# Laying softmax factors along the columns by way of DRAM instead of by transposes, in one layer of a hybrid encoder

## The chip, the cores and the metric

The kernel runs on one core of a Trainium2 chip. A core has five engines with instruction queues of their own: TensorE (matmuls and transposes; PE in the profile, its weight loads PEld), VectorE (DVE), ScalarE (ACT), GpSimd (POOL) and SyncE (SP), which here only issues transfers. Transfers between DRAM and the core's memory run beside the engines, on 16 DMA engines. The metric is the device time of one execution in microseconds (us). A result is the median of several executions.

## The reference

One layer on a sequence of 512 positions and a model width of 1024, batch 1, all in float32:

```python
h = rms_norm(x, attn_norm_g)
xr, gate, q, k, v = split(h @ w_in)
y_rnn = (rg_lru(conv(xr), forward) + rg_lru(conv(xr), backward)) * gelu(gate)
y_attn = dilated_attention(q, k, v, rel_bias)         # 8 heads of width 64
x = x + concat(rms_norm(y_rnn), rms_norm(y_attn)) @ w_out
x = x + square(relu(rms_norm(x) @ w_up)) @ w_down
return rms_norm(x)
```

The dilated attention has three windows with different strides; the outputs of the three are combined by the denominators of their softmaxes. That is the same as one softmax over all 512 keys with a bias per distance that counts how many windows hold the key. For each head and each query, the sum of the exponentials is the denominator; its reciprocal is the softmax factor that this change is about.

## The kernel before

**Matmuls.** Every float32 matmul is done as three: both operands are split into a rounded part and a remainder (`..h`/`hi` and `..l`/`lo`), and high x high, high x low and low x high are added (`mm3`, lines 303 to 305). Weights come in chunks of 128 x 1024: a transfer fills one of three buffers `wraw` (line 234, issued by SyncE), ScalarE makes `whi` (line 251), VectorE the remainder `wlo` (line 259), and the next `wraw` load goes out when the buffer is free.

**Stages.** Input projection with the recurrent group's gates and scans (to about 90 us); the attention loop, with the rest of the projections and the first half of the output projection woven in (to about 192 us); the second half of the output projection (to about 219 us); then the up and down projections in two halves, with products saved by sums and differences of blocks, and the final norm.

**The attention loop** (lines 1009 to 1041) goes over `i` from 0 to 4 and over four query blocks `u`. Heads are taken in pairs, `p` = 0 to 3. In step `i`, TensorE computes the scores of pair `i` (`att_s`, tiles `ps`; lines 754, 755) and turns the exponentials of pair `i-1` (`att_t`, tiles `pt`, line 778). VectorE adds the bias to the scores and takes the minimum (`att_e`, line 767), ScalarE takes the exponential and the sum over the keys (line 768). The bias comes from `tw` tiles, loaded by `load_tw` (line 450). Between these, `fill` runs "fillers": the key and query projections of the later pairs (tiles `pqk`) and then the output projection of the recurrent group (tiles `pwo`). The products with the values (`att_av`, tiles `pav`, line 859) run for pair 0 at the start of `i` = 2, for pairs 1 and 2 at the start of `i` = 4, and for pair 3 after the loop.

**The softmax factors.** `att_e` gathers the sums of the exponentials of a pair in a tile of 128 x 8: the query within its block is the partition, and the eight columns are four blocks times two heads. The products `pav` lie the other way: the 64 value columns of each of the two heads are the partitions, and the 512 queries the columns. So the factors must be laid along the columns and repeated over 64 partitions. Before, that is done so:

- `att_z` (at `u` = 0, lines 789 and 791): VectorE takes the reciprocal `rz` and repeats each of its columns 64 times, `rzb`, 128 x 512.
- `att_r` (at `u` = 1, lines 382 and 798): TensorE transposes `rzb` in four pieces into one PSUM bank, `prow`, and ScalarE copies it to `zrow`.
- `att_av` (line 863): VectorE multiplies `pav` by `zrow`, tile `yp`. For pairs other than 2, `att_q` and `att_a` follow at once on ScalarE; for pair 2 they come later by a plan (`att_a` at `i` = 4, `u` = 1).

**What sets the order.** TensorE, VectorE, ScalarE and GpSimd run their instructions in the order of the program's statements. SyncE does not: its transfers are ordered by the framework's planner, which sends them as what they need is expected to be ready, and SyncE then runs its queue in that order, waiting at each for its semaphores. Tiles of 128 x 512 come from a pool of 48 (`g_`); small ones from pools of 8.

At the end of the key projections, in step `i` = 2, `load_x` sends the residual (`x`, eight transfers) and the pre-added blocks of the output weights (`ws`: four transfers by SyncE, on which GpSimd adds seven more by accumulating transfers, line 948).

Of the kernel before, what the change touches and what calls it, by code (L numbers as in the profile page):

```python
# [12 lines left out]
FT = mybir.dt.float32  # L13
FR = mybir.dt.float32r
AF = mybir.ActivationFunctionType
OP = mybir.AluOpType

P = 128
S = 512
# [3 lines left out]
DH = 64  # L23
# [76 lines left out]
def hybrid_kernel(ctx: ExitStack, tc, xw, xn, w_in, w_v, w_out, w_up, w_dn, gates, vecs, rel, onehot, fg, out):  # L100
    nc = tc.nc
# [4 lines left out]
    dram = ctx.enter_context(tc.tile_pool(name="dram", bufs=1, space=bass.MemoryType.DRAM))  # L106
# [3 lines left out]
    act = nc.scalar.activation  # L110
# [3 lines left out]
    def g_(name, dt=FT, shape=(P, S)):  # L114
        return work.tile(list(shape), dt, name=name, tag="g", bufs=NG)

    def small(name, w):
        return work.tile([P, w], FT, name=name, tag="sm%d" % w, bufs=8)
# [256 lines left out]
    def fan(t, c, n, w):  # L375
        base = t[:, c:c + 1]
        return bass.AP(tensor=base.tensor, offset=base.offset, ap=[base.ap[0]] + ([[1, n]] if n > 1 else []) + [[0, w]])

    def rows_of(cols, tag):
        pr = ps_("prow", tag)  # L380
        for tt in range(4):
            nc.tensor.transpose(pr[:, tt * P:(tt + 1) * P], cols(tt), ident)
        return pr
# [63 lines left out]
    def load_tw(h):  # L447
        t = work.tile([P, 1024], FT, name="tw", tag="tw", bufs=4)[:, :896]
        ap = bass.AP(tensor=nbd.tensor, offset=nbd.offset + h * 2 * S, ap=[[1, P], [1, 896]])
        nc.sync.dma_start(t, ap)  # L450
        tws[h] = t
# [293 lines left out]
    et, en, zs = {}, {}, {}  # L745
# [3 lines left out]
    def att_s(p, qt):  # L749
        c0 = P * qt  # L750
        psq[p] = [ps_("ps", "gs") for _ in range(2)]
        for e in range(2):
            q = sp[p, 0, "h", e][:, c0:c0 + P]
            nc.tensor.matmul(psq[p][e], lhsT=q, rhs=sp[p, 1, "h", e], start=True, stop=False)
            nc.tensor.matmul(psq[p][e], lhsT=q, rhs=sp[p, 1, "l", e], start=False, stop=True)

    def att_e(p, qt):
        if qt == 0:
            en[2 * p], en[2 * p + 1] = [], []
            zs[p] = small("zz", 8)  # L760
        pss = psq.pop(p)
        c0 = P * qt
        for e in range(2):
            h = 2 * p + e
            t = g_("e")
            mn = small("mn", 1)
            nc.vector.tensor_tensor_reduce(t, pss[e], tws[h][:, c0:c0 + S], 1.0, 3.0e38, OP.add, OP.min, mn)
            act(t, t, AF.Exp, scale=-1.0, bias=mn, accum_out=zs[p][:, 2 * qt + e:2 * qt + e + 1])
            en[h].append(t)
        if qt == 3:  # L770
            for e in range(2):
                del sp[p, 0, "h", e], sp[p, 1, "h", e], sp[p, 1, "l", e]
            del tws[2 * p], tws[2 * p + 1]

    def att_t(h, jt):
        pt = ps_("pt", "et")
        for qt in range(4):
            nc.tensor.transpose(pt[:, qt * P:(qt + 1) * P], en[h][qt][:, jt * P:(jt + 1) * P], ident)  # L778
        t = g_("ett")
        act(t, pt, AF.Copy)  # L780
        et[h, jt] = t
        if jt == 3:
            del en[h]

    pav, zrow, rzbs = {}, {}, {}

    def att_z(p):
        rz = small("rz", 8)
        nc.vector.reciprocal(rz, zs.pop(p))
        rzb = g_("rzb")  # L790
        nc.vector.tensor_copy(rzb, fan(rz, 0, 8, DH))
        rzbs[p] = rzb

    def att_r(p):
        rzb = rzbs.pop(p)
        pr = rows_of(lambda tt: rzb[:, tt * P:(tt + 1) * P], "et")
        zrow[p] = g_("zrow")
        act(zrow[p], pr, AF.Copy)

    def att_y(p):  # L800
        y_add(1)
# [50 lines left out]
    def att_av(p, jts):  # L852
        if 0 in jts:
            pav[p] = ps_("pav", "gs" if p else "pj")
        for jt in jts:
            for e in range(2):
                a = slice(64 * e, 64 * e + 64)
                h = 2 * p + e
                nc.tensor.matmul(pav[p][a, :], lhsT=vs[:, jt, h * DH:(h + 1) * DH], rhs=et.pop((h, jt)),  # L859
                                 start=jt == 0, stop=jt == 3)  # L860
        if 3 in jts:
            y = g_("yp")
            nc.vector.tensor_tensor(y[:, ::-1], pav.pop(p), zrow.pop(p), op=OP.mult)
            yat[p] = y
            if p != 2:
                att_q(p)
                att_a(p)
# [56 lines left out]
    def fill(n):  # L924
        for _ in range(n):
            if fillers and fillers[0] is None:
                fillers.popleft()
                load_x()
            if fillers:
                fillers.popleft()()  # L930
# [57 lines left out]
    def beside(*key):  # L988
        for e in plan.pop(key, ()):
            e()  # L990
# [18 lines left out]
    for i in range(5):  # L1009
        for u in range(4):  # L1010
            if i < 4:
                att_s(i, u)
                if u == 0 and i < 3:
                    load_tw(2 * i + 2)
                if u == 2 and i < 3:
                    load_tw(2 * i + 3)
            if i >= 1:
                att_t(2 * i - 2, u)
                att_t(2 * i - 1, u)
            if i < 4:  # L1020
                att_e(i, u)
            if u == 0 and i >= 1:
                att_z(i - 1)
            if u == 0:
                for p in AVS.get(i, ()):
                    att_av(p, range(4))
            beside(i, u, 0)
            fill(FILL.get((i, u), (1, 1, 1, 1))[0])
            beside(i, u, 1)
            fill(FILL.get((i, u), (1, 1, 1, 1))[1])  # L1030
            if u == 1 and i >= 1:
                att_r(i - 1)
            if u == 0:
                for p in AVS.get(i, ()):
                    if p != 2:
                        att_y(p)
            beside(i, u, 2)
            fill(FILL.get((i, u), (1, 1, 1, 1))[2])
            beside(i, u, 3)
            fill(FILL.get((i, u), (1, 1, 1, 1))[3])  # L1040
            beside(i, u, 4)
# [598 lines left out]
```

## Time and profile before

| what | value |
|---|---|
| median of 3 executions | 543.67 us (543.66 to 544.35) |
| profiled execution | 544.4 us, span 542.2 us |
| TensorE busy | 533.5 us, 98% of the span |
| VectorE busy | 431.6 us, 80% |
| ScalarE busy | 363.4 us, 67% |
| GpSimd busy | 64.1 us, 12% |
| granted TensorE clock | 0.997 of full speed |
| transferred | 106.96 MB, mean 197 GB/s |

The span is the time from the first to the last instruction in the profile; the profiled execution's own time is somewhat longer. "Busy" is the time in which an engine had an instruction in work. The chain is followed back from the last instruction, at each step to what released it. A row of a group names the line, the engine, the operation, the tiles (written <- read), the shape, the number of instructions and their times; a row of a timeline begins with the start and the length in us, and an idle time in brackets names what ended it. In the rows of queues, q1 carries SyncE's transfers, q10 ScalarE's and q0 GpSimd's; the numbers are packets, MB, and the time of the packets as a share of 16 engines' time in the stretch asked for. A transfer's "landing" is the time from its issue to its completion.

### The profile page before, as it was taken

The page shows a single profiled execution, that of the slowest core. Times are in us where ns is not written, and L with a number is a line of the kernel's source. Part 1 is how long each engine was busy: PE and PEld are TensorE (multiplying, and loading weights), DVE is VectorE, ACT ScalarE, POOL GpSimd, SP SyncE. Part 2 cuts the span into 40 slices and gives each one's busy share as a digit, 9 for nine tenths or more (in the row PEclk, how much of TensorE's full clock was granted, in tenths as well). Part 3 has the DMA queues.
Part 4 walks back from the last instruction along what each step waited for, and adds up shares of the span by engine and source line. Part 5 has one row for each costly group of instructions (what it writes and reads, how often), then busy time and mean ns, then how long its engine had stood idle before and what let it go on. Part 6 is the DMA issues. An engine that isn't in the chain of part 4 may idle for free.

```text
span 542.2 us, 8156 instructions
## 1 busy us (share of the span) xinstructions
PE 533.5 (98%) x3018; PEld 452.9 (84%) x3018; DVE 431.6 (80%) x628; ACT 363.4 (67%) x573; POOL 64.1 (12%) x91
## 2 busy tenths in 40 slices
PE   9999999999999999999999999999999999999994
PEld 7856888887887578889999888888999999888883
DVE  6897788996673599889769987879755888886984
ACT  7667983798774755677566855565645777755665
POOL 3330000000001031001030223001001020131000
PEclk9999999999999999999999999999999999999998
DMA  7754276454398788855676799994987397799704
GB/s 273 230 163 142 54 246 182 132 180 143 83 343 215 178 152 204 296 202 160 192 156 167 204 253 273 284 366 104 283 236 205 113 191 199 195 283 262 191 1 157
DMA packets 34360, 106.96 MB, mean 197 GB/s; under 512 B 4228, under 2 KB 5124, under 8 KB 34320
## 3 DMA queue, kind: packets, MB, share of 16 engines
q1 hardware_dynamic: 25600, 76.56, 41.4%
q0 software_dynamic: 7968, 28.76, 28.4%
q10 hardware_dynamic: 752, 1.12, 0.6%
q8 instruction: 24, 0.39, 0.3%
q14 instruction: 16, 0.13, 0.1%
HBM read 98.00 MB, written 4.23 MB: 189 GB/s over the span
## 4 chain that ended last, share of the span: by engine, by line
PE 87%; DVE 4%; ACT 4%; DMA 3%; issue 1%; ACTq 0%; DVEq 0%
PE pd L304 8%; PE pd L303 8%; PE pd L305 8%; PE pu L305 7%; PE pu L303 7%; PE pu L304 7%; PE pqk L303 3%; DMA tw<-in_w_up_dram 3%; PE pwo L303 3%; PE pqk L305 3%; PE pqk L304 3%; PE pav L859 3%; PE pt L778 3%; PE pwo L305 3%; PE pwo L304 3%; DVE wlo L259 2%
## 5 line engine op out<-in xcount | busy, mean ns | idle before, releaser
L259 DVE TENSOR_TENSOR wlo<-wraw,whi 128x1024 fp32r<-128x1024 f32 x73 | 89.0, 1221 | 21.4 <-ACT whi L251 21.1
L251 ACT ACTIVATE whi<-wraw 128x1024 fp32r<-128x1024 f32 x70 | 74.0, 1059 | 34.6 <-PE pd L305 19.5
L303 PE MATMUL pd<-whi,ah 128*128 128x512 f32 x192 | 74.7, 389 | 0.0
L304 PE MATMUL pd<-wlo,ah 128*128 128x512 f32 x192 | 74.7, 389 | 0.0
L305 PE MATMUL pd<-whi,al 128*128 128x512 f32 x192 | 74.7, 389 | 0.0
L251 ACT ACTIVATE whi<-tw 128x1024 fp32r<-128x1024 f32 x36 | 38.0, 1059 | 40.0 <-DMA tw<-in_w_up_dram 13.3
L304 PE MATMUL pu<-hl,whi 128*128 128x256 f32 x224 | 63.4, 283 | 0.0
L305 PE MATMUL pu<-hh,wlo 128*128 128x256 f32 x224 | 63.4, 283 | 0.0
L303 PE MATMUL pu<-hh,whi 128*128 128x256 f32 x224 | 63.4, 283 | 0.0
L305 PE MATMUL pu<-h2h,wlo 128*128 128x256 f32 (+1 forms) x200 | 60.1, 301 | 0.6 <-DVE wlo L259 0.6
L303 PE MATMUL pu<-h2h,whi 128*128 128x256 f32 (+1 forms) x200 | 60.1, 300 | 0.0
L304 PE MATMUL pu<-h2l,whi 128*128 128x256 f32 (+1 forms) x200 | 60.0, 300 | 0.0
L259 DVE TENSOR_TENSOR wlo<-tw,whi 128x1024 fp32r<-128x1024 f32 x36 | 44.0, 1223 | 19.5 <-ACT whi L251 19.5
L303 PEld LDWEIGHTS pu<-hh,whi 128*128 128x128 f32 x224 | 43.0, 192 | 0.0
L304 PEld LDWEIGHTS pu<-hl,whi 128*128 128x128 f32 x224 | 43.0, 192 | 0.0
L305 PEld LDWEIGHTS pu<-hh,wlo 128*128 128x128 f32 x224 | 43.0, 192 | 0.0
L251 ACT ACTIVATE whi<-ts 128x1024 fp32r<-128x1024 f32 x24 | 25.5, 1061 | 25.3 <-PE pd L305 18.3
L303 PEld LDWEIGHTS pd<-whi,ah 128*128 128x128 f32 x192 | 36.0, 188 | 7.5
L305 PEld LDWEIGHTS pd<-whi,al 128*128 128x128 f32 x192 | 36.0, 188 | 7.5
L304 PEld LDWEIGHTS pd<-wlo,ah 128*128 128x128 f32 x192 | 36.0, 188 | 7.4
L305 PEld LDWEIGHTS pu<-h2h,wlo 128*128 128x128 f32 x200 | 38.2, 191 | 2.1 <-DVE wlo L259 0.8
L304 PEld LDWEIGHTS pu<-h2l,whi 128*128 128x128 f32 x200 | 38.3, 191 | 1.3
(261 smaller groups left out, 1262.8 us busy)
## 6 DMA issues: line engine op xcount, KB each, us to landing
wraw<-in_w_up_dram SPq DMA_DIRECT2D x25, 512.0 KB, 4.1
ts<-in_w_dn_dram POOLq DMA_DIRECT2D x24, 512.0 KB, 13.9
wraw<-in_w_dn_dram SPq DMA_DIRECT2D x24, 512.0 KB, 9.2
tw<-in_w_up_dram SPq DMA_DIRECT2D x15, 512.0 KB, 9.9
tw<-in_w_up_dram POOLq DMA_DIRECT2D x15, 512.0 KB, 7.8
wraw<-in_w_in_dram SPq DMA_DIRECT2D x13, 512.0 KB, 3.5
ts<-in_w_dn_dram SPq DMA_DIRECT2D x8, 512.0 KB, 5.0
tw<-in_w_dn_dram SPq DMA_DIRECT2D x8, 512.0 KB, 8.0
```

The lines of the kernel that those rows point to most:

```text
L251: act(hi, raws[i], AF.Copy)
L259: nc.vector.tensor_tensor(lo, r, f(splits[i][0]), op=OP.subtract)
L303: nc.tensor.matmul(o, lhsT=a[0], rhs=b[0], start=bool(first), stop=False, skip_group_check=on)
L304: nc.tensor.matmul(o, lhsT=a[0], rhs=b[1], start=False, stop=False, skip_group_check=on)
L305: nc.tensor.matmul(o, lhsT=a[1], rhs=b[0], start=False, stop=bool(last), skip_group_check=on)
L778: nc.tensor.transpose(pt[:, qt * P:(qt + 1) * P], en[h][qt][:, jt * P:(jt + 1) * P], ident)
L859: nc.tensor.matmul(pav[p][a, :], lhsT=vs[:, jt, h * DH:(h + 1) * DH], rhs=et.pop((h, jt)), start=jt == 0, stop=jt == 3)
```

## The change

For pairs 0, 1 and 2 the repeated tile `rzb`, the four transposes and the copy are left out. `att_z` takes the reciprocal only. `att_zw`, stated at `u` = 1, writes the 128 x 8 factors to a DRAM tile of 2 x 512, each number to its place (head, query); the columns of the sums are ordered head by head for that. `att_zr`, stated at `u` = 3, reads the two rows of that tile back, each of them repeated over 64 partitions, into `zrow`. Both transfers are SyncE's. Pair 3 goes as before.

```diff
-            act(t, t, AF.Exp, scale=-1.0, bias=mn, accum_out=zs[p][:, 2 * qt + e:2 * qt + e + 1])
+            z = 4 * e + qt if p < 3 else 2 * qt + e
+            act(t, t, AF.Exp, scale=-1.0, bias=mn, accum_out=zs[p][:, z:z + 1])
...
+    zd = {}
+
+    def att_zw(p):
+        zd[p] = dram.tile([2, S], FT, name="zd%d" % p)
+        t = zd[p]
+        nc.sync.dma_start(bass.AP(tensor=t.tensor, offset=t.offset, ap=[[1, P], [P, 8]]), rzs.pop(p))
+
+    def att_zr(p):
+        t = zd[p]
+        zrow[p] = g_("zrow")
+        nc.sync.dma_start(zrow[p], bass.AP(tensor=t.tensor, offset=t.offset, ap=[[S, 2], [0, DH], [1, S]]))
+
+    rzs = {}
+
     def att_z(p):
         rz = small("rz", 8)
         nc.vector.reciprocal(rz, zs.pop(p))
+        if p < 3:
+            rzs[p] = rz
+            return
         rzb = g_("rzb")
...
             if u == 1 and i >= 1:
-                att_r(i - 1)
+                att_zw(i - 1) if i < 4 else att_r(3)
+            if u == 3 and 1 <= i < 4:
+                att_zr(i - 1)
```

## The prediction

> **What bounds the kernel now.** I read the page first (engines, chain of waits), then the stretches of the attention stage engine by engine, then the chain there in order of time.
>
> ```profile
> span 542.2 us, 8156 instructions
> PE 533.5 (98%) x3018; PEld 452.9 (84%) x3018; DVE 431.6 (80%) x628; ACT 363.4 (67%) x573; POOL 64.1 (12%) x91
> PE 87%; DVE 4%; ACT 4%; DMA 3%; issue 1%; ACTq 0%; DVEq 0%
> sum 115.00, PE 114.87 PEld 87.89 DVE 85.80 ACT 80.09 POOL 12.07; mean PE 19.15 PEld 14.65 DVE 14.30 ACT 13.35 POOL 2.01
> 120.00 0.44 PE prow L382 x4
> 143.31 0.44 PE prow L382 x4
> 161.91 0.44 PE prow L382 x4
> 183.17 0.44 PE prow L382 x4
> ```
>
> TensorE carries 87% of the chain. The fourth row sums the stretches from 100 to 215 us, the attention loop and what follows it: TensorE is busy 114.87 of 115.00 us, so there every matmul removed moves the end, and every wait added to TensorE does too. The last four rows, from the chain in order of time, are the four groups of transposes of the softmax factors. The first three are those that the change takes out; the fourth (pair 3) stays.
>
> **The change part by part.** Durations are from the profiled execution: 544.4 us by its own clock, a span of 542.2 us plus 2.2 us around it. It stands 0.7 us above the median, 543.67 us; I take differences from the profile and apply them to the median. A change below about 0.2%, 1.09 us, can't be told from none.
>
> *Transposes out.* Three groups on the chain at 0.44 us each: 3 x 0.44 = 1.32 us gained, 0.88 us of it before the third pair's work begins. This is also the most that can be gained, as nothing else removed is on the chain:
>
> ```profile
> L791 DVE COPY rzb<-rz x4: 426/426/427, 114.7 to 172.5; 128x512 f32<-128x512 f32 x4
> L798 ACT ACTIVATE zrow<-prow x4: 584/591/597, 121.4 to 183.6; 128x512 f32<-128x512 f32 x4
> ```
>
> Three of each go: 1.3 us of VectorE and 1.8 us of ScalarE, in a stage in which they are busy 86 and 80 of 115 us. I count them at nothing. The column order of the exponentials' sums (4e+qt) changes an address alone: nothing.
>
> *The writes in.* Each is 128 partitions x 8 numbers that go to places 512 bytes apart, so 1,024 pieces of 4 bytes, 64 for each of 16 transfer engines. No row shows such a piece. The nearest are the queue that carries small rows:
>
> ```profile
> q10 hardware_dynamic: 144, 0.03, 1.7%
> q10 hardware_dynamic: 752, 1.12, 0.6%
> nbd<-nbs ACTq DMA_DIRECT2D x2, 16.0 KB
> vt<-in_vecs_dram ACTq DMA_DIRECT2D x1, 34.0 KB
> out_dram<-ot ACTq DMA_DIRECT2D x4, 256.0 KB, 2.8
> ```
>
> The first is that queue from 0 to 12 us, where it carries the 34 KB of `vt` alone: 1.7% x 16 x 12 us / 144 = 23 ns a packet. The second is the whole span: 0.6% x 16 x 542.2 / 752 = 69 ns. A write takes 64 x 23 = 1.5 to 64 x 69 = 4.4 us of every engine; both rows are far from a 4-byte write to DRAM, so I take the middle, 2.9 us. A gain below nothing is excluded, since no transfer is removed.
>
> *The reads in.* 128 rows of 2 KB. Their source pattern counts 2 x 64 x 512, with the 2 outermost. How many engines share a transfer can be counted in the rows above: the four outputs have 512 data packets, `vt` 128, the two `nbs` writes (8 rows each) 16, in all 656 of 752. The other 96 are closing packets, and 5 x 16 + 2 x 8 = 96: the two transfers whose outermost count is 8 ran on 8 engines. By that, a read with 2 outermost runs on 2 engines, 64 rows each. [...] By that rule the sum is the 546.0 us below, without it the 542.35 us of the first rival.
>
> ```profile
> q1 hardware_dynamic: 258, 0.40, 45.8%
> q0 software_dynamic: 26, 0.11, 51.6%
> q1 hardware_dynamic: 44, 0.18, 50.8%
> ```
>
> The first row is 118.6 to 122.6 us, with two key copies of 2 KB rows alone: 45.8% x 16 x 4.0 / 258 = 114 ns a packet. 64 rows on one engine are 7.3 us; spread over 16 engines they would be 8 rows, 0.9 us. The other two are 483.0 to 484.1 us, with GpSimd's accumulating queue and SyncE's both full: each has half of the engines' time, and a packet of the accumulating one takes 51.6% x 16 x 1.1 / 26 = 0.35 us. [...]
>
> *Where each lands.* SyncE issues in the order in which things come ready, not in that of the statements: `load_t` stands after the attention loop and goes out inside it, at 156.18.
>
> ```profile
> 116.88 1.12 SPq L731 DMA_DIRECT2D kh<-kh  x2
> 119.36 1.18 SPq L739 DMA_DIRECT2D kl<-kl  x2
> 148.33 4.47 SPq L942 DMA_DIRECT2D x<-in_xn_dram  x8
> 156.18 14.23 SPq L1046 DMA_DIRECT2D tw<-in_w_up_dram  x4
> 171.22 0.33 SPq L234 DMA_DIRECT2D wraw<-in_w_up_dram  x1
> 114.52 0.20 DVE L789 RECIPROCAL rz<-zz 128x8 f32<-128x8 f32 x1
> 134.01 0.20 DVE L789 RECIPROCAL rz<-zz 128x8 f32<-128x8 f32 x1
> 136.31 0.69 DVE L863 TENSOR_TENSOR yp<-pav,zrow 128x512 f32<-128x512 f32 x1 [1.64 <-PE pav L859]
> 177.32 0.69 DVE L863 TENSOR_TENSOR yp<-pav,zrow 128x512 f32<-128x512 f32 x1 [4.44 <-PE pav L859]
> 131.81 0.88 PE pt L778 x8
> ```
>
> Pair 0: the reciprocal ends at 114.7; write to about 118, read to about 125, with another 2 us for each landing 129; the product wants it at 136.3. Hidden, 7 us of cover. SyncE is held at the read until the write has landed, and behind it stand the next pair's key copies (116.88, 119.36), whose rows on the read's engines then queue behind its 64. They are wanted just ahead of the transposes at 131.8; I take nothing, and price it among the rivals. Pair 1: from 134.2, read landed by 142 to 149; its product comes only at 177.32. The `x` loads from 148.3 may find two engines busy for a microsecond. Nothing.
>
> Pair 2 is another matter, because its write falls into the densest stretch of transfers:
>
> ```profile
> tw<-in_w_up_dram SPq DMA_DIRECT2D x2, 512.0 KB, 12.0
> 155.95 0.20 DVE L789 RECIPROCAL rz<-zz 128x8 f32<-128x8 f32 x1
> 168.89 2.69 POOL L948 DMA_DIRECT2D ws<-in_w_out_dram  x3 [8.48 <-DMA ws<-in_w_out_dram]
> 180.75 0.69 DVE L863 TENSOR_TENSOR yp<-pav,zrow 128x512 f32<-128x512 f32 x1 [2.74 <-PE pav L859]
> 184.88 0.43 DVE L838 TENSOR_TENSOR osum<-at 128x256 f32<-128x256 f32 x1 [1.71 <-ACT at L874]
> 193.19 0.69 DVE L575 TENSOR_TENSOR ysq<-ysq 128x512 f32<-128x512 f32 x1 [0.70 <-ACT ysq L569]
> PEld pcs L402 <- DVE ysq L575: 0.4, 1, 0.4
> ```
>
> The reciprocal ends at 156.15, about when the two `tw` loads go out on the same queue, behind 2 MB of `x`, 2 MB of `ws` and one `wraw`. Those two land 12.0 us later, at 168.2; with the 0.88 us already gained, 167.3. The write moves behind them: 167.3 + 2.9 = 170.2. Then the read: 7.3 us, and at each turn one of the 3 x 8 accumulating packets per engine that GpSimd has issued from 168.89: 24 x 0.35 = 8.4 us. It lands at 170.2 + 7.3 + 8.4 = 185.9.
>
> Its product is wanted at 180.75 - 0.88 = 179.9, so it is 6.0 us late. VectorE waits in order: behind the product stand an addition, the `wlo` of the output weights, and from 184.88 on a run of work without idle time in which 1.71 and 0.70 us are the only gaps, up to the addition at 193.19 for which TensorE's column sums already wait (last row). So TensorE loses 6.0 - 1.71 - 0.70 = 3.6 us. On ScalarE the scaling of that product and the copies of pair 3's transposes behind it are late by less.
>
> Sum: 3.6 - 1.3 = 2.3 us slower, 543.67 + 2.3 = 546.0 us. Bounds of the third pair's term: with 23 ns pieces and no turns given to GpSimd the read lands at 167.3 + 1.5 + 7.3 = 176.1 and costs nothing; with 69 ns pieces and, for both transfers, the 2.2 us that a key copy needs from issue to landing, at 167.3 + 4.4 + 7.3 + 8.4 + 4.4 = 191.8, which is 9.5 us of TensorE and 8.2 us net, 551.9 us.
>
> ```profile
> kl<-kl SPq DMA_DIRECT2D x2, 128.0 KB, 2.2
> ```
>
> SyncE held until 170 by the read delays the last two of the four `tw` and the `wraw` of 171.22 by some microseconds; these are weights of the stage after and are three buffers ahead. If that cover is gone, ScalarE's `whi` waits for a `wraw`, as long as the load is late.
>
> **The rivals.**
>
> *All of it hidden.* If the third write goes out ahead of the two `tw` loads, or the read is spread over 16 engines, the read lands before 180: 0.9 us in place of 7.3, with 2 to 3 turns of GpSimd's in place of 24 (170.2 + 0.9 + 1.1 = 172.2). Then the whole 1.32 us stays: 542.35 us, 0.24% faster. For it: pairs 0 and 1 have it in any case, and no row shows a transfer on 2 engines. Against: the closing packets, and an issue order by readiness, in which the `tw` slots (freed with the last minimum at 155.95) come just before the reciprocal's end. It decides at a lateness of 2.4 us.
>
> *Late, but by little.* With a lateness of 2.6 to 4.8 us, loss and gain cancel: 542.6 to 544.7 us. It needs a packet time a quarter below mine.
>
> *Slow small writes.* If a 4-byte write costs some 0.2 us a piece, three times my upper row, a write is 13 us of every engine. Pair 0's read then lands at 114.7 + 13 + 7.3 = 135, still in time for its product, but SyncE holds the key copies until 128 and they queue behind the read until 135, against 131.8: TensorE loses 3 us there, and the third pair lands at 196, 14 us of it lost. About +15 us, 559 us. A milder form, at 69 ns and with landing times of 2.2 us: the key copies come at 113.4 + 3.3 + 4.4 + 2.2 + 7.3 + 2.2 = 132.8 us, 1 to 2 us late.
>
> ```profile
> 113.40 0.33 SPq L234 DMA_DIRECT2D wraw<-in_w_out_dram  x1
> wraw<-in_w_out_dram SPq DMA_DIRECT2D x3, 512.0 KB, 3.3
> ```
>
> (113.4 is the `wraw` load ahead of that write, 3.3 us its landing.)
>
> **How the numbers follow.** Third read late by more than 4.8 us, key copies late or not: 0.40, slower. Late by little: 0.17, within 0.2%. Hidden: 0.35, faster by 0.24%, just beyond what can be told. Slow small writes: 0.08, slower. So faster 0.35, same 0.17, slower 0.48. The predicted time is the first case's. The range starts at the hidden case, 542.2, and ends at 550.0, which leaves out the slow writes and the far end of the late read; the first case's own range is 544.8 to 551.9.
>
> **What would show it.** Three of the four `prow` groups gone from the chain, nine tenths of a microsecond earlier at 150 us. In the groups, `zrow` read from DRAM with a landing near 9 us for pairs 0 and 1 (2 engines) or near 3 us (16). At the third product, VectorE idle for several microseconds with the transfer `zrow` as the releaser, and TensorE idle at `pcs` or at a `pt` soon after. If the third product still waits for `pav`, the step of the late read is wrong and the time is 542.35; if `ps` waits for `kl` in pair 2, the key copies were caught behind the read.

## The result, and the profile after

The changed kernel takes 560.94 us (557.98 to 562.55, 6 executions) where the kernel before takes 543.66 us (543.09 to 544.35, 6 executions): ratio 1.0309, 95% interval 1.0286 to 1.0333. It is 17 us slower, and lies outside the predicted range of 542.2 to 550.0 us. The profiled execution was 562.55 us. The experiments below are given as ratios to the kernel before, run on the same chip; one per cent is 5.4 us.

First the page of the changed kernel: span, engines, granted clock in 40 slices, and the chain.

```profile
span 560.4 us, 8135 instructions
PE 537.6 (96%) x3006; PEld 455.0 (81%) x3006; DVE 430.4 (77%) x625; ACT 362.6 (65%) x570; POOL 63.5 (11%) x91
PEclk9999999999799979999999999999999999999999
PE 85%; DMA 7%; DVE 2%; ACT 2%; SPq 1%; issue 1%; ACTq 0%; DVEq 0%
```

The span grew by 560.4 - 542.2 = 18.2 us. TensorE's idle time went from 542.2 - 533.5 = 8.7 us to 560.4 - 537.6 = 22.8 us, which is 14.1 us of it. The other 4.1 us are *busy* time: TensorE does fewer matmuls than before (3006 against 3018) and needs longer for them. The two 7s in the clock's row, the slices of 140 to 154 and 196 to 210 us, say why.

The waits of the changed kernel between 100 and 230 us (engine, line and tile, what it waited for; total, times, longest):

```profile
DVE yp L883 <- DMA zrow<-zd: 15.2, 1, 15.2
ACT whi L251 <- DMA ws<-in_w_out_dram: 9.8, 1, 9.8
DVE yp L883 <- issue: 10.3, 1, 10.3
PE pt L779 <- ACT ett L781: 8.6, 2, 6.6
PE pt L779 <- DVE rv L387: 5.7, 1, 5.7
```

TensorE waited three times, 5.7 + 8.6 = 14.3 us in all, each time at `pt`, the transposes of exponentials. VectorE had two long waits, both at `yp`, the product with the factors. The second is put down to the read of the factors, the first to "issue", that is, to nothing that the profile can name. The timelines of SyncE and VectorE show which products these are and what SyncE did before them (start, length):

```profile
114.94 0.37 SPq L795 DMA_DIRECT2D zd<-rz  x1
117.10 3.83 SPq L731 DMA_DIRECT2D kh<-kh  x2
128.32 0.63 SPq L800 DMA_DIRECT2D zrow<-zd  x1
134.00 0.37 SPq L795 DMA_DIRECT2D zd<-rz  x1
144.26 0.69 DVE L883 TENSOR_TENSOR yp<-pav,zrow 128x512 f32<-128x512 f32 x1 [10.29 <-issue]
168.66 0.76 SPq L795 DMA_DIRECT2D zd<-rz  x1
186.19 0.54 SPq L800 DMA_DIRECT2D zrow<-zd  x1
200.76 0.69 DVE L883 TENSOR_TENSOR yp<-pav,zrow 128x512 f32<-128x512 f32 x1 [15.22 <-DMA zrow<-zd]
```

Pair 0: the write went out at 114.94, the read at 128.32, and the product, at 136.31 before, ran at 144.26. Pair 1's write was issued at 134.00, while pair 0's read was under way. Pair 2: write at 168.66, read at 186.19, product at 200.76 (before: 180.75).

The chain in order of time shows what each of these delays did to TensorE:

```profile
141.27 2.99 issue
147.00 1.11 PE pt L779 x4
148.11 0.43 PE pqk L303
168.66 17.48 DMA zd<-rz
186.19 14.48 DMA zrow<-zd
200.76 0.70 DVE yp L883
201.49 0.72 ACT at L894
202.21 0.49 ACT ett L781
202.75 1.97 PE pt L779 x8
204.72 0.43 PE pwo L303
211.62 0.23 PE pwo L305
```

At pair 2 the chain is write (17.48 us), read (14.48 us), product, ScalarE's `at` and `ett`, and then TensorE's transposes. After both stalls the 512-column matmuls take 0.43 us each instead of 0.23, and eight transposes 1.97 us instead of 0.88: TensorE runs at about half speed after it has stood still for about 6 us, from 147.0 to 152.9 and from 202.7 to at least 207.3 us. That is the additional busy time: 4.1 us, or 5.4 us with the 1.3 us of transposes that went away. At pair 0 the chain has VectorE's work behind the late product (144.26), which `pt` at 147.00 waits for. The shortest of the three waits, 1.96 us at 191.09, comes before the late product of pair 2: there ScalarE had waited 9.8 us for the output weights `ws`.

Last, where the small pieces were. Of the changed kernel, the packets of 116 to 117 us, SyncE's queue at 139 to 140 and at 144 to 145 us (packets, MB, share of 16 engines), and from 110 to 135 us the landings of the key copies and of the first two writes:

```profile
DMA packets 949, 0.11 MB, mean 114 GB/s; under 512 B 922, under 2 KB 922, under 8 KB 949
q1 hardware_dynamic: 3, 0.00, 94.9%
q1 hardware_dynamic: 128, 0.00, 7.2%
kh<-kh SPq DMA_DIRECT2D x2, 128.0 KB, 9.7
kl<-kl SPq DMA_DIRECT2D x2, 128.0 KB, 6.4
zd<-rz SPq DMA_DIRECT2D x2, 4.0 KB, 11.4
```

922 packets under 512 bytes, nearly as many as the write has pieces (1,024), moved within one microsecond, yet the write landed 11.4 us after its issue. The key copies behind it took 9.7 and 6.4 us, against 2.2 before. The second row is the queue at the time when pair 0's product waits: three packets with 94.9% x 16 x 1 us = 15.2 us of engine time, some 5 us each, and nothing else started until 144 us. They are not rows of the read, which have 2 KB: two are small, and the third has 4 KB, as a row of the `wraw` load issued at 132.70 us, behind the read. From 138 us on no packet of 2 KB started at all. The third row, at 144 us, is 128 small packets, as many as two engines' share of pair 1's write (64 each). So, by that count, 14 engines' share of that write was out by 138 us, and the share of two came only at 144 us; what kept the read, whose rows had moved, from counting as landed, the profile does not show.

### The profile page after: what moved, and what is told of

Its sections match the earlier page's. It is cut to its first block, busy times and chain, and to the rows that moved or that the text cites. A ratio compares the mean times of both kernels' runs of the same rounds, so it can differ in the third digit from the quotient of the medians.

```text
span 560.4 us, 8135 instructions
## 1 busy us (share of the span) xinstructions
PE 537.6 (96%) x3006; PEld 455.0 (81%) x3006; DVE 430.4 (77%) x625; ACT 362.6 (65%) x570; POOL 63.5 (11%) x91
## 3 DMA queue, kind: packets, MB, share of 16 engines
q1 hardware_dynamic: 29110, 77.36, 41.9%
## 4 chain that ended last, share of the span: by engine, by line
PE 85%; DMA 7%; DVE 2%; ACT 2%; SPq 1%; issue 1%; ACTq 0%; DVEq 0%
PE pu L303 10%; PE pu L304 10%; PE pu L305 10%; PE pd L305 8%; PE pd L303 8%; PE pd L304 8%; DMA zd<-rz 3%; PE pqk L303 3%; PE pqk L304 3%; PE pqk L305 3%; DMA zrow<-zd 3%; PE pwo L303 2%; PE pt L779 2%; PE pg L489 1%; PE pwo L305 1%; PE pwo L304 1%
## 5 line engine op out<-in xcount | busy, mean ns | idle before, releaser
L303 PEld LDWEIGHTS pu<-h2h,whi 128*128 128x128 f32 x200 | 38.3, 191 | 1.3
```

Source lines behind the costliest of these rows:

```text
L303: nc.tensor.matmul(o, lhsT=a[0], rhs=b[0], start=bool(first), stop=False, skip_group_check=on)
```

## The experiments

**No factors at all.** The bare gain: reciprocals stay, writes and reads are left out.

```diff
-            nc.vector.tensor_tensor(y[:, ::-1], pav.pop(p), zrow.pop(p), op=OP.mult)
+            nc.vector.tensor_tensor(y[:, ::-1], pav.pop(p), zrow.pop(p, rstd), op=OP.mult)
...
-                att_zw(i - 1) if i < 4 else att_r(3)
-            if u == 3 and 1 <= i < 4:
-                att_zr(i - 1)
+                rzs.pop(i - 1) if i < 4 else att_r(3)
```

> Leaves the softmax factors of pairs 0 to 2 out: no write, no read, and the products of these pairs are multiplied by a tile that is there anyway, so the values are not the layer's. All theories: nothing waits for a transfer, three groups of transposes at 0.44 us are gone, 1.3 us faster than the kernel before, about 542.3 us. If it is within 0.5 us of the kernel before, the transposes were not on the path and the step of the gain falls.

Measured: 542.51 us, ratio 0.9976 (0.9966 to 0.9986). That is 1.3 us less than before, as the three groups of transposes summed to.

**The write alone.** As before, with the line of `att_zw` kept: the writes go out and nobody reads them.

> The three writes in 4-byte pieces are made, the reads are left out and the products use a tile that is there anyway (values not the layer's). Small-write theory: the key copies issued behind a write land 6 to 10 us after their issue in place of 2.2, yet nothing that TensorE needs comes late enough; 542.3 to 545 us. Two-engine-read theory: the writes do no harm, 542.3 us, key copies at 2 to 3 us. Neither expects a stall of 5 us.

Measured: 548.58 us (two executions, 547.37 and 549.79), ratio 1.0091 (1.0061 to 1.0120). Both theories had at most 545 us. Of this kernel, the landings of `zd` (least, median, most), GpSimd's first wait for the output weights `ws`, ScalarE's wait for them, and the chain:

```profile
DMA to landing us min/median/max: 11.2/12.6/17.1
174.66 2.68 POOL L968 DMA_DIRECT2D ws<-in_w_out_dram  x3 [15.28 <-DMA ws<-in_w_out_dram]
ACT whi L251 <- DMA ws<-in_w_out_dram: 11.3, 1, 11.3
158.39 15.97 DMA ws<-in_w_out_dram
174.66 7.11 DMA ws<-in_w_out_dram
183.39 1.97 PE pt L779 x8
```

The same two waits of the kernel without factors:

```profile
168.84 2.72 POOL L968 DMA_DIRECT2D ws<-in_w_out_dram  x3 [8.68 <-DMA ws<-in_w_out_dram]
ACT whi L251 <- DMA ws<-in_w_out_dram: 8.6, 1, 8.6
```

The writes land as late as in the changed kernel, without any read, and they cost time with no one waiting for them. The output weights `ws`, accumulated by GpSimd's own queue, come later: GpSimd waits 15.28 us for the first of them, against 8.68 without factors. ScalarE then waits 11.3 us for `ws`, against 8.6, so `pt` comes late, TensorE stands still for 3.4 us instead of 0.8, and the slow clock follows (busy 533.6 us against 532.2). In the two profiled executions this is 545.3 - 541.4 = 3.9 us of the span. Between the medians it is 548.58 - 542.51 = 6.1 us, but the first is that of two executions, 2.4 us apart, and the profile is of the shorter. A write that only its own reader was to feel holds up transfers of another queue.

This is no fixed price. The kernel with the read on 16 engines, further down, makes the same writes and is only 544.35 - 542.51 = 1.8 us slower than the one without factors: there pair 2's write goes out at 158.92 us instead of 155.04, and GpSimd's first wait for `ws` is 10.19 us.

**The write in runs of 32 bytes.** Same bytes, same queue, the read as in the change.

```diff
-        nc.sync.dma_start(bass.AP(tensor=t.tensor, offset=t.offset, ap=[[1, P], [P, 8]]), rzs.pop(p))
+        nc.sync.dma_start(bass.AP(tensor=t.tensor, offset=t.offset, ap=[[8, P], [1, 8]]), rzs.pop(p))
```

> The write goes out as 128 runs of 32 bytes, one per partition, in place of 1,024 pieces of 4 bytes (so the factors lie in the wrong order and the values are not the layer's); the reads stay as they are, on two engines. Small-write theory: the write lands in about 3 us and no longer holds what is behind it; what is left is the read of 64 rows on each of two engines, 7 to 9 us for pair 0 and some 15 us among GpSimd's transfers for pair 2: 546 to 552 us. Two-engine-read theory: hardly better than the changed kernel, 556 to 561 us.

Measured: 548.57 us, ratio 1.0092 (1.0076 to 1.0109): 12 us of the 17 are gone. The key copies land in 2.2 us again, pair 0's product runs at 138.39. What is left is pair 2, in the chain of this kernel:

```profile
160.23 13.15 DMA zd<-rz
173.43 14.18 DMA zrow<-zd
187.70 0.70 DVE yp L883
189.68 1.97 PE pt L779 x8
```

The read on two engines still takes 14.18 us in this stretch. The write of pair 2, 128 runs now, also stays long (13.15 us, with the residual, the weights and `tw` in flight). As such a write lands in 2.2 us on a quiet queue (pair 0 in the run with both changes, below), the full queue is the likely reason here.

**The read on 16 engines.** The same two rows, read in two transfers of 64 partitions each, so that the partitions are outermost; the write in 4-byte pieces.

```diff
-        nc.sync.dma_start(zrow[p], bass.AP(tensor=t.tensor, offset=t.offset, ap=[[S, 2], [0, DH], [1, S]]))
+        for e in range(2):
+            nc.sync.dma_start(zrow[p][halves[e]], bass.AP(tensor=t.tensor, offset=t.offset + e * S, ap=[[0, DH], [1, S]]))
```

> The read is made as two transfers, one for each head, each onto 64 partitions with these outermost on both sides, so that 16 engines can share it; the writes stay in 4-byte pieces. Two-engine-read theory: the read takes 2 to 4 us and nearly all of the loss goes, 543 to 547 us. Small-write theory: the writes still land 11 to 17 us after their issue, pair 0's read is still held until the next pair's write has landed, and pair 2's read goes out some 17 us after the write: 550 to 558 us.

Measured: 544.35 us, ratio 1.0016 (1.0001 to 1.0032): 16 us of the 17 are gone. Of this kernel, the landings of `zrow`, and the third product:

```profile
DMA to landing us min/median/max: 4.2/5.7/8.1
185.47 0.69 DVE L884 TENSOR_TENSOR yp<-pav,zrow 128x512 f32<-128x512 f32 x1 [8.39 <-DMA zrow<-zd]
```

The read lands in 4.2 to 8.1 us. Over the whole span SyncE's queue has 29,200 packets, against 29,110 in the change and 28,720 with the writes alone: beside its 128 rows each read has 32 small packets here and 2 in the change, which agrees with one from each of 16 engines for either of its transfers, and from each of 2 in the change. Pair 0's product runs at 136.31 and no longer waits for a transfer. Pair 2's still does, since its write took 17.8 us, but this costs TensorE only some 0.8 us, at `pcs` (196.63). Its idle time of 1.8 us, at 182.51, is before that product: ScalarE had waited 9.7 us for `ws`. After both the clock stayed at 1.00. Each of the two theories met one of the last two runs and missed the other.

**Both.** 32-byte runs and two reads of 64 partitions.

> Both at once: the write in 128 runs of 32 bytes (wrong order of the factors, values not the layer's) and the read as two transfers on 16 engines. If small pieces and the two-engine read are the whole loss, every product finds its factors: pair 2's write, in the queue behind the residual and the weights, lands about 13 us after its issue as in the run with 32-byte runs, the read takes some 4 us more, 178 against 179.5 wanted, and the three groups of transposes are gone: 542.3 to 543.5 us. If the path by DRAM itself (a write landed before the read is sent, on a queue full of loads) costs, it is still 544 to 547 us.

Measured: 541.58 us, ratio 0.9957 (0.9941 to 0.9972). No product waits for a transfer. Of this kernel, the row of 175 to 195 us in the table by stretches (length, then busy time of TensorE, its weight loads, VectorE, ScalarE, GpSimd; granted clock, DMA share, GB/s):

```profile
175.00:195.00 20.00, 20.00 (x108) 12.20 (x105) 13.64 (x26) 13.19 (x26) 3.73 (x4) 1.00 0.81 191
```

The four kernels side by side (ratio to the kernel before):

| | read on 2 engines | read on 16 engines |
|---|---|---|
| 4-byte pieces | 1.0309 (the change) | 1.0016 |
| 32-byte runs | 1.0092 | 0.9957 |

Against the last of them, the pieces alone cost 0.0059, the two engines alone 0.0135, and both together 0.0352. The excess over the sum is 0.0158, 8.6 us: the two make each other worse.

**Is pair 0's read held by pair 1's write?** Two runs ask this. In the first, only pair 0 goes by way of DRAM, the other pairs by transposes.

```diff
-            z = 4 * e + qt if p < 3 else 2 * qt + e
+            z = 4 * e + qt if p in (0,) else 2 * qt + e
...
-        if p < 3:
+        if p in (0,):
...
-                att_zw(i - 1) if i < 4 else att_r(3)
-            if u == 3 and 1 <= i < 4:
+                att_zw(i - 1) if i - 1 in (0,) else att_r(i - 1)
+            if u == 3 and i - 1 in (0,):
```

> Only pair 0 goes by DRAM, in the changed kernel's way (4-byte pieces, read on two engines); pairs 1 and 2 are turned by transposes. If pair 0's read is held by the write of pair 1 issued behind it, that write is now gone and the product starts near 138, as with 32-byte runs: at most 2 us of VectorE's waiting, 543.5 to 546 us. If the read is slow by itself, the product still starts near 144, TensorE idles some 5.7 us and runs at half clock for some 6 us after: 550 to 553 us.

Measured: 546.02 us, ratio 1.0040 (1.0022 to 1.0059). Of this kernel, the first product, the stretch of 135 to 155 us, and SyncE's queue from 136 to 138 us:

```profile
139.29 0.69 DVE L883 TENSOR_TENSOR yp<-pav,zrow 128x512 f32<-128x512 f32 x1 [4.69 <-DMA zrow<-zd]
135.00:155.00 20.00, 18.02 (x96) 14.07 (x93) 12.14 (x25) 13.59 (x26) 1.05 (x1) 1.00 0.40 113
q1 hardware_dynamic: 49, 0.10, 13.0%
```

The product runs at 139.29, not at 144.26, TensorE loses 2 us, and its clock stays full. The third row is that read, alone on the queue: 13.0% of 16 engines is 2.1 engines, so it runs on two, and 49 packets in 13.0% x 16 x 2 us = 4.2 us are 85 ns each, 5.4 us for the 64 rows of an engine.

In the second run all is as in the change, but pair 1's write goes in 32-byte runs.

```diff
-        nc.sync.dma_start(bass.AP(tensor=t.tensor, offset=t.offset, ap=[[1, P], [P, 8]]), rzs.pop(p))
+        ap = [[8, P], [1, 8]] if p == 1 else [[1, P], [P, 8]]
+        nc.sync.dma_start(bass.AP(tensor=t.tensor, offset=t.offset, ap=ap), rzs.pop(p))
```

> As the changed kernel, but the write of the second pair alone goes as 128 runs of 32 bytes instead of 1,024 pieces of 4 bytes; the writes of the first and third pair and all three reads are unchanged. The second pair's factors lie in the wrong order, so its values are not the layer's. Theory (the first pair's read is done in time, and the second pair's write of small pieces, queued right behind it, holds back its landing): the first pair's product starts near 138 to 139 us of the span instead of 144, TensorE's first stall shrinks from 5.7 us to 2 us or less with no stretch of half clock behind it, and the kernel takes 552 to 554 us. Rival (the first pair's read is late by itself, held only by its own write before it): the product still starts near 144 us and the time stays near 560 us.

Measured: 552.52 us, ratio 1.0172 (1.0144 to 1.0200). Of this kernel, the first product, and the stretch of 135 to 155 us; for comparison, the same stretch of the changed kernel:

```profile
138.63 0.69 DVE L884 TENSOR_TENSOR yp<-pav,zrow 128x512 f32<-128x512 f32 x1 [4.33 <-PE pqk L305]
135.00:155.00 20.00, 20.00 (x108) 16.02 (x105) 14.75 (x30) 14.26 (x30) 1.05 (x1) 1.00 0.57 173
```

```profile
135.00:155.00 20.00, 14.26 (x64) 11.10 (x61) 8.38 (x17) 7.65 (x15) 1.05 (x1) 0.83 0.39 78
```

The first stall is gone, idle time and slow clock both. (The product is still 2 us later than in the kernel before; the matmul that its row names as the releaser is not one that it needs, and the time is about that of the run with pair 0 alone.) One write of 4 KB, of another pair and issued *after* the read, is worth 0.0137, 7.4 us. That is near the 8.6 us by which the two causes exceed their sum; how much of it belongs to that excess, no run separates.

**Pair 2 alone.** As with pair 0 alone, with `p in (2,)`.

> Only pair 2 goes by DRAM, in the changed kernel's way. Its write falls into the loads of the residual and of the output weights: it lands some 17 us after its issue, the read goes out then and takes some 14 us on two engines among GpSimd's transfers, so the product comes 6 to 15 us late: 548 to 555 us. If pairs 0 and 2 lose independently, its loss and that of the run with pair 0 alone add up to the changed kernel's 17 us; if they hold each other up, they add up to less.

Measured: 553.85 us, ratio 1.0170 (1.0135 to 1.0206). Of this kernel, the longest waits of ScalarE for weights and of VectorE for the factors from 155 to 215 us (total, times, longest):

```profile
ACT whi L251 <- DMA ws<-in_w_out_dram: 14.8, 2, 13.6
DVE yp L883 <- DMA zrow<-zd: 5.3, 1, 5.3
```

The third pair alone costs more than half of the loss, and here more through the weights than through its product: the product waits 5.3 us and runs at 182.91, ScalarE waits 13.6 us for `ws`. Pair 0 alone loses 1.9 us and pair 2 alone 9.7 us, together 11.6 of the 17.3 us. The rest comes only with pair 1, or when the pairs meet.

**Count of pieces, or shared rows?** The write alone again, but with the eight pieces of a partition 8 bytes apart in 64 bytes of its own.

```diff
-        zd[p] = dram.tile([2, S], FT, name="zd%d" % p)
+        zd[p] = dram.tile([4, S], FT, name="zd%d" % p)
-        nc.sync.dma_start(bass.AP(tensor=t.tensor, offset=t.offset, ap=[[1, P], [P, 8]]), rzs.pop(p))
+        nc.sync.dma_start(bass.AP(tensor=t.tensor, offset=t.offset, ap=[[16, P], [2, 8]]), rzs.pop(p))
```

> The write alone, as in the run with the write only: the three writes of 1,024 pieces of 4 bytes stay and nothing reads them; the products take the plain rstd tile instead of the factor, so the values are not the layer's. Here the eight pieces of one partition lie 8 bytes apart inside one 64-byte stretch of memory that no other partition writes to, instead of one in each of eight rows of 512 bytes that all partitions share. Theory (what costs is the count of pieces): the writes still land 11 us or more after their issue, the weights' reads still wait, and the time stays near 548 us. Rival (what costs is that several transfer engines write into the same short stretch of memory): the writes land within 3 to 6 us and the time is 542.5 to 545 us.

Measured: 546.25 us (543.99 to 547.54), ratio 1.0036 (1.0020 to 1.0052), between the two theories. The landings of `zd`, which were 11.2, 12.6 and 17.1 us with the pieces in shared rows:

```profile
DMA to landing us min/median/max: 6.8/7.0/12.4
```

With as many pieces, the places alone shorten the landing by about 5 us. Between the medians they save some 2.3 of the 6.1 us that the write costs, and 546.25 - 542.51 = 3.7 us remain; these two shares are rough, as the write alone ran only twice, and this kernel's ten executions spread over 3.6 us. So both theories hold in part.

**A version that beats both.** The 128 x 8 factors are turned once (one transpose of 0.27 us, a copy of 0.25 us), so that the write has eight runs of 512 bytes, and read on 16 engines.

```diff
+        pr = ps_("prow", "et")
+        nc.tensor.transpose(pr[0:8, 0:P], rzs.pop(p), ident)
+        zt = g_("zt", shape=(8, P))
+        act(zt, pr[0:8, 0:P], AF.Copy)
-        nc.sync.dma_start(bass.AP(tensor=t.tensor, offset=t.offset, ap=[[1, P], [P, 8]]), rzs.pop(p))
+        nc.sync.dma_start(bass.AP(tensor=t.tensor, offset=t.offset, ap=[[P, 8], [1, P]]), zt)
...
-        nc.sync.dma_start(zrow[p], bass.AP(tensor=t.tensor, offset=t.offset, ap=[[S, 2], [0, DH], [1, S]]))
+        for e in range(2):
+            nc.sync.dma_start(zrow[p][halves[e]], bass.AP(tensor=t.tensor, offset=t.offset + e * S, ap=[[0, DH], [1, S]]))
```

> The layer's values. One transpose of the 128 x 8 factors into 8 rows of 128, a copy by ScalarE, a write of 8 runs of 512 bytes, and the read as two transfers on 16 engines; the four wide transposes and the wide copy are out. A quarter of the transposes stays: at most 3 x 0.33 = 1.0 us gained, 542.7 us, if everything lands in time; the theory of small pieces and two engines expects that. If the queue's load alone makes pair 2 late, 544 to 547 us.

Measured: 542.02 us (541.55 to 542.45), ratio 0.9953 (0.9941 to 0.9966): 2.1 us below the 544.13 us of the kernel before on that chip. Its page:

```profile
span 540.0 us, 8150 instructions
PE 532.1 (99%) x3009; PEld 451.8 (84%) x3009; DVE 430.5 (80%) x625; ACT 363.1 (67%) x573; POOL 63.9 (12%) x91
```

TensorE is busy 1.4 us less than before and idle 540.0 - 532.1 = 7.9 us, 0.8 us less. Of the latter, 0.6 us is one wait of the up projection for a `wlo`, between 400 and 500 us, that the kernel before has and this one has not.

## Why the prediction was wrong, point by point

**The direction and the gain were right.** "Three groups on the chain at 0.44 us each": the kernel without factors gained 1.3 us, 1.32 predicted. "This is also the most that can be gained" was too strict: by their intervals, the two versions with quick transfers lie 1.5 to 3.2 us below before. In the version with one transpose 0.8 us of that is idle time, most of it a wait in another stage.

**The step that failed is "A write takes ... I take the middle, 2.9 us".** It priced a write by what its pieces occupy. That was even high: most pieces moved within 1 us. What a write costs is its landing, 11.4 us for pair 0, and what it does to the landings around it. With the writes alone mended, in 32-byte runs, the kernel takes 548.57 us, inside the predicted range. From this step follow the other errors:

- *"Pair 0 ... Hidden, 7 us of cover."* The read went out at 128.32, where I had it landed by 129. Alone, the product then ran 3 us late (139.29 against 136.31), with pair 1's write behind the read 8 us late. I had looked at what a transfer is queued behind, and never at what is queued behind *it*; "Pair 1 ... Nothing" left out that pair 1's write meets pair 0's read. The run with pair 1's write in 32-byte runs puts 7.4 us on this.
- *The weights.* That `ws`, on GpSimd's queue, could come later because of a 4 KB write on SyncE's was in no term and no rival. In the run with the write alone this is the whole loss, 3.9 us in the profile and 6.1 us between medians.

**The step on the two engines was right,** and by more than it was given credit for. It was carried over from two transfers with 8 outermost; the runs showed it for 2: on the queue the read fills 2.1 of 16 engines, and cutting it into two transfers gave back 16 us. Alone on the queue its 64 rows take 5.4 us and not 7.3: the 114 ns a packet behind the 7.3 were a mean over 258 packets, of which 63 were small. The sum for pair 2 nearly holds where its write is in larger runs. There the read took 14.18 us, against 7.3 + 8.4 = 15.7, and the product ran at 187.70, where I had the landing at 185.9. That was partly two errors that cancel: the write went out behind one of the `tw` loads and not two, at 160.23 instead of 167.3, and took 13.15 us instead of 2.9. That the 8.4 us are turns given to GpSimd's packets no run shows: in the row behind the 0.35 us, 26 of its packets moved beside 44 of SyncE's, not one for one. What was measured in its place is 14.18 us for this read among the other loads and 5.4 us alone.

**What follows from a late product was mis-sized, and on the wrong path.** "TensorE loses ... 3.6 us" was worked out by way of VectorE and the column sums `pcs`. ScalarE was said to be "late by less". But the chain goes by ScalarE: the product, `at`, `ett`, `pt`; ScalarE runs in order, and the copies of pair 3's transposed exponentials (`ett`) stand behind the scaled output of pair 2 (`at`). In the run with 32-byte runs the loss is 548.57 - 542.51 = 6.1 us, for a product 187.70 - 179.26 = 8.4 us later than in the kernel without factors (predicted: 3.6 us for 6.0). A term for the slow clock after a stall was missing altogether; it is 537.6 - 532.2 = 5.4 us of the changed kernel's loss, measured against TensorE's busy time without factors.

**The rivals.** "All of it hidden" fell with the two engines and returned as soon as both transfers were mended. "Slow small writes" had 559 us for 560.94, but its mechanism did not happen: the pieces do not fill the engines for 13 us, the key copies landed by 128 and were in time for 131.8, and the first stall is at pair 0's *product*. Its number is near because it, too, let a write take over 10 us and hold what lies behind it, and otherwise by luck; its chance of 0.08 was too low.

**What stays open.** Why a write of 4-byte pieces lands so late is shown only in part: pieces in 64-byte places of their own land in 7.0 us, in shared rows in 12.6 (medians), as 32-byte runs in 2.2 (pair 0). How pair 1's write reaches back to a read issued 5.7 us before it is not visible. The trace shows that the read's rows had moved by 138 us, that the last packets of the load behind it took some 5 us each, and that the product ran at 144.26 us, when the rest of the write set out.

## What to carry to other kernels

Price a transfer by its landing and by what shares its engines at that time, not by the time that its bytes take; a DRAM write of scattered 4-byte pieces is not a small transfer (4 KB landed here after 10.3 to 17.8 us), and here it delayed a transfer issued before it (the product behind pair 0's read ran at 144.26 us, and at 138.63 with pair 1's write in 32-byte runs) and transfers on another queue (GpSimd waited 15.28 us for `ws` with the writes alone, 8.68 without factors). Put the partitions outermost in a repeating read, in two transfers if need be: here that took the change from 560.94 to 544.35 us. Where a stall of TensorE is forecast to be as long as those that slowed it here, 3.4 us and more, add 1 to 3 us for the slow matmuls after it: here they cost 1.2 us (32-byte runs), 1.4 us (write alone) and 2.7 us for each of the two stalls of the change.

## What the runs showed of the hardware

**Small pieces to DRAM.** 1,024 pieces of 4 bytes in shared rows landed after 10.3 to 17.8 us, though most moved within one microsecond (922 small packets from 116 to 117 us in the change), and key copies behind them landed after 6.4 and 9.7 us instead of 2.2. With the writes alone, on SyncE's queue, the weights on GpSimd's came later: GpSimd's first wait for `ws` was 15.28 us, against 8.68 without factors. What links the two queues no run shows. It is not simply a wait for the write to land: with the read on 16 engines, the first of these loads was there at 170.6 us and pair 2's write only at 176.7. Nor do the runs show how pair 1's write, issued after pair 0's read, holds that read up. Pieces in places of their own landed 5.6 us sooner (medians, 7.0 against 12.6 us); the reason is not shown either.

**Half speed after a stall.** Idle times of TensorE of 5.7 and 6.6 us (the change), 4.8 (32-byte runs) and 3.4 us (write alone) were each followed by matmuls of 0.43 us instead of 0.23; after 1.8 us (read on 16 engines) and 2 us in all (pair 0 alone) the granted clock stayed at 1.00. What an idle time between 2 and 3.4 us does is not shown. Full speed was back after 3.2 us of work (write alone, 183.4 to 186.6) to 5.9 us (the change, 147.0 to 152.9).
